# Layer two of a feed-forward block: a sixth Strassen-Winograd product split into seven inner ones, weight differences made together, some sums on GpSimd

## The chip, the cores and the metric

One core of a Trainium2 chip runs the whole program. The metric is device time in microseconds of one launch, the median of several runs. One further execution was taken with the hardware profiler; every duration below is from it.

## The reference

A decoder block on 2048 tokens of width 1024 in float32: an input projection, two token mixers, an output projection, and a feed-forward block. Only the feed-forward block is touched:

```python
hn2 = rmsnorm(h, norm2_g)
up = jnp.einsum('bsd,df->bsf', hn2, w_up)        # 1024 -> 4096
act = jnp.square(jax.nn.relu(up))
h = h + jnp.einsum('bsf,fd->bsd', act, w_down)   # 4096 -> 1024
return rmsnorm(h, final_g)
```

## The kernel before

Precision comes from splitting: `split` writes a high part (ScalarE, a rounding copy) and the remainder (VectorE, a subtraction) of a tile, and each product is three matmuls (high x high, high x low, low x high). One matmul is 128x128 stationary by 128x512 moving.

Both layers use Winograd's form of Strassen's scheme: the matrices are cut in two by two blocks, and seven products P1 to P7 of sums and differences of blocks take the place of eight. The operands on the activations' side are A11, A12, A22, S1, S2, S3, S4; those on the weights' side are b11, b12, b21, b22 and the differences t1, t2, t3 (t1 = b12 - b11, t3 = b22 - b12, t2 = b21 - (b22 - t1), in the kernel's indices).

Layer one (`up`) runs over 32 columns (q, m): q is the half of the tokens, m one of 16 blocks of 128 outputs. A column is seven slots, one product each, of 4 x 3 matmuls into one of the banks X, Y, Z. `make_weights` splits a slot's weights UA = 4 slots ahead, `post` takes the products out of the banks, applies relu and square, and stores the seven operands of layer two, each in `sd[q][i]` (i numbers the operand), by DMAs on SyncE's queue. In the second half of the columns (q = 1), `inner_row` loads the first half's operand again, and `inner_sums` forms inner sums of the operands in INNER and stores them in `sdi[i]`; all of them are made on VectorE. Per pair of columns and operand these are four operations of 128x512: one in the first column (line L886), three in the second (L891, L893, L895).

Layer two (`down`) goes through the products in the order P1, P6, P7, P4, P5, P2, P3. P1, P6 and P3 are plain: 8 blocks of the inner dimension for each half of the tokens, 4 x 6 matmuls each (L1452). P7, P4, P5 and P2 are split again (`SPLIT`): each becomes seven inner products by the same scheme, of 4 steps of 12 matmuls (L1275), so 28 steps and 336 matmuls for 384. A split product needs the inner sums `sdi[i]` of its activation operand (four sums) and the inner differences `wi[i]` of its weight operand (P5, P7, P6, P4), both read back from DRAM. `make` prepares a step ahead: a DMA of the row tile `ar` (128x1024), a split into `ad`, and for each second step a weight tile `wr` or `wq`, split into `wd`; at most six rows and three weight tiles stand ahead of TensorE in the program. The pools hold five `ar` tiles, five `ad` tiles, three `wd` tiles.

Where the weight operands come from: `weights_first` runs in the first half of layer one, a piece at a time at slots chosen by column, and makes first t1 and its inner differences, later t3 and its own, on VectorE (L997, L1003). The rest is made in layer two: the inner differences of b21 (A12) at some steps of P1, P7 and P5, and in P6, where b22 - t1 is P6's own plain weight operand (`minus`, L1166), t2 is made from it, stored, and differenced (L1157). Those run late, through the list `late`.

Instructions of each engine stand in a fixed order that a list scheduler with a time line of its own has set; every engine works through its own order, and so does SyncE's queue, which issues nearly all DMAs. The residual is added by DMAs from GpSimd's queue that accumulate into the result (`add_residual`, L1250).

```python
slots += [c + (s,) for s in ("P2", "P6", "P5", "P7")]
slots += [c2 + ("P1",) for c2 in cols[n + 1:n + 2]]
slots += [c + (s,) for s in ("P4", "P3")]
...
while ahead[0] < limit and (ahead[1] + lefts(ahead[0]) <= 6 and ahead[2] + stationary(ahead[0]) <= 3):
    make(ahead[0])
```

Of the kernel before, what the change touches and what calls it, by code (L numbers as in the profile page):

```python
# [46 lines left out]
def hymba_block(ctx: ExitStack, tc: tile.TileContext, xT, gains, w_in, pool_w, w_out, w_up, w_down, out):  # L47
# [64 lines left out]
    for i in range(PAD):  # L112
# [24 lines left out]
    sdi = {i: [[dram.tile([P, 2, T], F32, name=f"sdi{i}_{n}_{c}") for c in range(4)] for n in range(4)] for i in (1, 2, 3, 5)}  # L137
    wi = {i: {n: [dram.tile([P, 4, 256], F32, name=f"wi{i}_{n}_{c}") for c in range(2)]
              for n in ("P5", "P6", "P7", "P4")} for i in (1, 2, 3, 5)}
    td = [[dram.tile([P, 4, 256], F32, name=f"td{i}_{c}") for c in range(8)] for i in range(3)]  # L140
# [720 lines left out]
    def up(pools, more):  # L861
# [6 lines left out]
        INNER, waiting = (A22, S1, A12, S3), []  # L868

        def inner_row(m, i):  # L870

            if m < NM // 2:
                t = srp.tile([P, 2, T], F32, tag="sr", name="hr") if i != S3 else None
# [4 lines left out]
        def inner_sums(m, i, t, now=False):  # L878
# [12 lines left out]
            nc.vector.tensor_tensor(a, a, t, ALU.add)  # L891
            keep(0, a)
            nc.vector.tensor_tensor(d, t, d, ALU.subtract)  # L893
            keep(1, d)
            nc.vector.tensor_tensor(r, r, d, ALU.subtract)  # L895
# [91 lines left out]
        def weights_first():  # L987

            for i, one, two, keep in ((S1, 1, 0, 0), (S3, 3, 1, 2)):
                for k in range(4):  # L990
                    b = {}
                    for x, y in ((0, 0), (0, 1), (1, 1), (1, 0)):
                        b[x, y], t = (avp.tile([P, 2, 256], F32, tag="av", name=n) for n in ("t1", "b11"))
                        nc.sync.dma_start(t, half(w_down[two, k + 4 * x], y))
                        nc.sync.dma_start(b[x, y], half(w_down[one, k + 4 * x], y))
                        yield
                        nc.vector.tensor_tensor(b[x, y], b[x, y], t, ALU.subtract)  # L997
                        if i == S1 or (x, y) != (0, 1):
                            nc.sync.dma_start(half(td[keep][k + 4 * x], y), b[x, y])
                        for to, u, v, p in {(0, 1): (((0, 0), (0, 1), (0, 0), "P5"),),  # L1000
                                            (1, 1): (((0, 1), (1, 1), (0, 1), "P7"), ((1, 1), (1, 1), (0, 0), "P6")),
                                            (1, 0): (((1, 0), (1, 0), (1, 1), "P4"),)}.get((x, y), ()):
                            nc.vector.tensor_tensor(b[to], b[u], b[v], ALU.subtract)  # L1003
# [114 lines left out]
    def down(pools):  # L1118
# [30 lines left out]
        def inner_weights(i, kk, t):  # L1149

            if kk < 4:
                tops[i] = t
                return
# [490 lines left out]
```

## Time and profile before

| | |
|---|---|
| Median of three runs | 1903.05 us (1901.46 to 1904.54) |
| The profiled execution | 1904.37 us, of which the span from the first to the last instruction is 1902.6 us |
| TensorE busy | 1879.0 us, 99% of the span |
| VectorE busy | 1481.2 us, 78% |
| ScalarE busy | 1025.2 us, 54% |
| GpSimd busy | 179.5 us, 9% |
| DMA | 535.91 MB, mean 282 GB/s |
| Layer one's first matmul, layer two's first | 694.4 and 1309.3 us after the span's start |

Matmuls are pipelined, so 99% busy doesn't mean that no time is lost: the time of a stage against the number of its matmuls tells that. GB/s is what the core's 16 DMA engines moved.

### The profile page before, as it was taken

To read this page: it belongs to the slowest core of one execution; us is meant where nothing else is said; L and a number is where in the kernel's file an instruction comes from. 1 tells how busy PE (TensorE), PEld (TensorE's weight loads), DVE (VectorE), ACT (ScalarE), POOL (GpSimd) and SP (SyncE) were. 2 spreads that over 40 slices of the span, in tenths; PEclk is the share of its full clock that TensorE was granted. 3 is DMA by queue.
4 is the path that set the end of the run, shared out by engine and by line. 5 is a ranking of instruction groups with operands and counts; after the bars stand their busy time and mean duration, and the time that the engine had idled before them with its cause. 6 is when DMAs were issued, how large, how long until landed. Compare 5 with 4: busy or idle time off the path is not lost.

```text
span 1902.6 us, 26763 instructions
## 1 busy us (share of the span) xinstructions
PE 1879.0 (99%) x8947; PEld 1568.1 (82%) x8947; DVE 1481.2 (78%) x2216; ACT 1025.2 (54%) x1616; POOL 179.5 (9%) x399
## 2 busy tenths in 40 slices
PE   9999999999999999999999999999999999999997
PEld 7888888888888888888888888887888888888886
DVE  6887799667966886878799988786666677888774
ACT  5565576555654465454557555554432665656543
POOL 0211123101211030000000000000010010020120
PEclk9999999999999999999999999999999999999998
DMA  6686596788888777787899888889999799999852
GB/s 220 204 273 197 193 297 223 241 311 266 288 314 306 265 266 243 281 313 273 299 359 338 311 293 287 303 282 334 383 314 337 276 317 309 329 300 335 290 209 91
DMA packets 222164, 535.91 MB, mean 282 GB/s; under 512 B 26048, under 2 KB 32192, under 8 KB 218176
## 3 DMA queue, kind: packets, MB, share of 16 engines
q1 hardware_dynamic: 217264, 525.46, 79.3%
q0 software_dynamic: 4608, 8.39, 2.5%
q8 instruction: 72, 1.18, 0.2%
q14 instruction: 76, 0.62, 0.1%
q10 hardware_dynamic: 144, 0.26, 0.0%
HBM read 349.46 MB, written 184.55 MB: 281 GB/s over the span
## 4 chain that ended last, share of the span: by engine, by line
PE 49%; DMA 5%; DVE 3%; ACT 1%; issue 1%; POOL 0%; SPq 0%; DVEq 0%; ACTq 0%
PE pb L1275 13%; PE pY L1102 13%; PE pb L1452 12%; PE pZ L1102 7%; PE pX L1102 3%; DMA ar<-sd 2%; DMA ar<-sdi 1%; PE pb L1392 1%; DMA wr<-in_w_down_dram 0%; DMA b<-in_w_down_dram 0%; DMA t<-in_w_down_dram 0%; DMA td<-t 0%; DMA hn<-hs 0%; DVE hw L147 0%; DMA su<-hs 0%
## 5 line engine op out<-in xcount | busy, mean ns | idle before, releaser
L1102 PE MATMUL pY<-sa,hw 128*128 128x512 f32 x1536 | 366.2, 389 | 1.0 <-ACT u L1025 1.0
L1102 PEld LDWEIGHTS pY<-sa,hw 128*128 128x128 f32 x1536 | 288.0, 188 | 61.8 <-ACT u L1025 2.1
L1275 PE MATMUL pb<-ad,wd 128*128 128x512 f32 x1344 | 305.4, 389 | 0.7 <-DVE ad L147 0.7
L178 PE MATMUL pd<-h,hl 128*128 128x512 f32 x752 | 299.6, 398 | 0.7 <-DVE qkr L424 0.7
L180 PE MATMUL pd<-h,hl 128*128 128x512 f32 x752 | 296.8, 395 | 0.0
L1275 PEld LDWEIGHTS pb<-ad,wd 128*128 128x128 f32 x1344 | 252.1, 188 | 53.9 <-DVE ad L147 1.6
L179 PE MATMUL pd<-h,hl 128*128 128x512 f32 x752 | 296.5, 394 | 0.0
L1452 PE MATMUL pb<-ad,wd 128*128 128x512 f32 x1104 | 253.6, 390 | 1.3 <-ACT ad L146 1.2
L1452 PEld LDWEIGHTS pb<-ad,wd 128*128 128x128 f32 x1104 | 206.6, 188 | 44.7 <-ACT ad L146 1.7
L147 DVE TENSOR_TENSOR ad<-ar,ad 128x1024 fp32r<-128x1024 f32 x160 | 194.2, 1222 | 41.9 <-ACT ad L146 41.3
L146 ACT ACTIVATE ad<-ar 128x1024 fp32r<-128x1024 f32 x160 | 168.3, 1053 | 93.7 <-PE pb L1452 35.4
L1102 PE MATMUL pZ<-sa,hw 128*128 128x512 f32 x768 | 186.5, 389 | 0.8 <-DVE a L1045 0.8
L1102 PEld LDWEIGHTS pZ<-sa,hw 128*128 128x128 f32 x768 | 144.0, 188 | 31.1 <-DVE a L1045 1.2
L178 PEld LDWEIGHTS pd<-h,hl 128*128 128x128 f32 x752 | 142.1, 189 | 28.1 <-DVE qkr L424 1.0
L180 PEld LDWEIGHTS pd<-h,hl 128*128 128x128 f32 x752 | 141.8, 189 | 28.0
L179 PEld LDWEIGHTS pd<-h,hl 128*128 128x128 f32 x752 | 141.8, 189 | 26.9
L146 ACT ACTIVATE hl<-raw 128x512 fp32r<-128x512 f32 x168 | 103.8, 630 | 109.4 <-PE pd L180 70.5
L147 DVE TENSOR_TENSOR hl<-raw,hl 128x512 fp32r<-128x512 f32 x168 | 114.3, 686 | 53.2 <-ACT hl L146 50.1
L1019 ACT ACTIVATE a<-a 128x512 f32<-128x512 f32 x96 | 60.1, 629 | 88.5 <-DVE a L1061 38.1
L147 DVE TENSOR_TENSOR hw<-rt,hw 128x512 fp32r<-128x512 f32 x128 | 86.7, 687 | 24.1 <-ACT hw L146 24.0
L146 ACT ACTIVATE wd<-wq 128x1024 fp32r<-128x1024 f32 x56 | 59.4, 1061 | 79.4 <-PE pb L1275 69.0
L147 DVE TENSOR_TENSOR wd<-wq,wd 128x1024 fp32r<-128x1024 f32 x56 | 68.5, 1224 | 34.3 <-ACT wd L146 34.3
(220 smaller groups left out, 2719.1 us busy)
## 6 DMA issues: line engine op xcount, KB each, us to landing
ar<-sd SPq DMA_DIRECT2D x96, 512.0 KB, 5.9
ar<-sdi SPq DMA_DIRECT2D x64, 512.0 KB, 5.6
rb<-in_w_up_dram SPq DMA_DIRECT2D x30, 1024.0 KB, 6.6
sd<-a SPq DMA_DIRECT2D x104, 256.0 KB, 5.1
raw<-in_w_in_dram SPq DMA_DIRECT2D x50, 512.0 KB, 4.6
sdi<-hr SPq DMA_DIRECT2D x96, 256.0 KB, 5.2
wr<-in_w_down_dram SPq DMA_DIRECT2D x48, 512.0 KB, 5.6
sd<-s SPq DMA_DIRECT2D x88, 256.0 KB, 4.7
```

Of the source, the lines that this page charges most:

```text
L146: nc.scalar.activation(hi, src, AF.Copy)
L147: return nc.vector.tensor_tensor(lo, src, hi.bitcast(F32), ALU.subtract)
L178: nc.tensor.matmul(ps, hl[:, 0, c], hi, start=(k == 0), stop=False)
L179: nc.tensor.matmul(ps, hl[:, 0, c], lo, start=False, stop=False)
L180: mm = nc.tensor.matmul(ps, hl[:, 1, c], hi, start=False, stop=(k == n - 1))
L1019: nc.scalar.activation(t, src, AF.Relu)
L1102: nc.tensor.matmul(t, w[:, wx, c], a[:, ax, c % 2], start=first and c == 0 and x == 0, stop=last and c == G - 1 and x == 2, skip_group_che ...
L1275: nc.tensor.matmul(b, t[:, wx, 2 * (kk % 2) + c, i * P:(i + 1) * P], a[:, ax, c], start=p in ("P1", "P5", "P2") and kk == 0 and c == 0 and ...
L1392: nc.tensor.matmul(b[:, cols], block(t, wx, c, n), a[:, ax, c, cols], start=False, stop=(i == 1 and c == 1 and x == 2), skip_group_check=True)
L1452: nc.tensor.matmul(ps[q, n], block(t, wx, c, n), left_[q][:, ax, c], start=(n_ in ("P1", "P3") and kk == 0 and c == 0 and x == 0), stop=(n ...
```

## The change

P6 is split like the other four. S2 joins INNER, so layer one also makes S2's inner sums; S2's and S3's are made on GpSimd, those of the other three stay on VectorE. `weights_first` now makes t1, t3 and t4 = b22 - t1 from one set of three loads in 16 units (three subtractions on VectorE, then the inner differences of all three on GpSimd). `down` makes t2 = b21 - t4 and the inner differences of b21 and t2 in four units of three parts (load; t2 and b21's; t2's) at the steps of the table TURNS. P1 now leaves both p1 and u2, P6 adds its parts to u2 and copies the sum to u3. The tile pool `avp` has 15 tiles for 13, paid for by one tile less of p1 and of u3; `rtx` is gone.

```diff
-        INNER, waiting = (A22, S1, A12, S3), []
+        INNER, waiting = (A22, S1, A12, S3, S2), []
...
+            engine = nc.gpsimd if i in (S2, S3) else nc.vector
...
-                nc.vector.tensor_tensor(d, d, t, ALU.subtract)
+                engine.tensor_tensor(d, d, t, ALU.subtract)
...
         def weights_first():
+            sub = lambda engine, to, x, y: engine.tensor_tensor(to, x, y, ALU.subtract)
+            KEEP = {S1: 0, S3: 2, S2: 3}
+            for k in range(4):
+                b = {}
+                for x, y in ((0, 0), (0, 1), (1, 1), (1, 0)):
+                    pair = srp.tile([P, 2, 2, 256], F32, tag="sr", name="tw")
+                    t = {S1: pair[:, 0], S3: pair[:, 1], S2: avp.tile([P, 2, 256], F32, tag="av", name="t2")}
+                    for i, at in ((S1, 0), (S3, 1), (S2, 3)):
+                        nc.sync.dma_start(t[i], half(w_down[at, k + 4 * x], y))
+                    yield
+                    sub(nc.vector, t[S1], t[S3], t[S1])
+                    sub(nc.vector, t[S3], t[S2], t[S3])
+                    sub(nc.vector, t[S2], t[S2], t[S1])
+                    for i in (S1, S3, S2):
+                        b[i, x, y] = t[i]
+                        if i == S2 or (x, y) != (0, 1):
+                            nc.sync.dma_start(half(td[KEEP[i]][k + 4 * x], y), t[i])
+                    yield
...
+                            sub(nc.gpsimd, to, u, v)
+                            nc.sync.dma_start(wi[i][p][k // 2][:, 2 * (k % 2):2 * (k % 2) + 2], to)
...
-            if s in (() if n == 0 else SUMS if n < 4 else ("P5", "P4") if n in (5, 7, 9, 11) else
-                     SUMS + ("P6", "P3") if 12 <= n < 16 else ()):
+            if s in (() if n == 0 or n > 13 else ("P2", "P5", "P4", "P3") if n in (3, 11, 12, 13) else ("P5", "P3")):
                 next(first_weights, None)
...
-        SPLIT = {"P7": S3, "P4": A22, "P5": S1, "P2": A12}
+        SPLIT = {"P6": S2, "P7": S3, "P4": A22, "P5": S1, "P2": A12}
...
+        TURNS = {4: (0, 0), 5: (1, 0), 6: (2, 0), 7: (0, 1), 10: (1, 1), 12: (2, 1), 22: (0, 2), 26: (1, 2), 29: (2, 2),
+                 40: (0, 3), 44: (1, 3), 47: (2, 3)}
+        def unit_weights(part, k):
+            sub = lambda to, x, y: nc.vector.tensor_tensor(to, x, y, ALU.subtract)
+            def differences(i, pair):
...
+                    sub(b[to], b[x], b[y])
+                    nc.sync.dma_start(wi[i][p][k // 2][:, 2 * (k % 2):2 * (k % 2) + 2], b[to])
+            if part == 0:
+                for name in ("b21", "t4"):
+                    unit[name] = rlp.tile([P, 2, 4, 256], F32, tag="rl", name=name)
+                    for x in range(2):
+                        nc.sync.dma_start(unit[name][:, x], w_down[2, k + 4 * x] if name == "b21" else td[3][k + 4 * x])
+            elif part == 1:
+                for x in range(2):
+                    sub(unit["t4"][:, x], unit["b21"][:, x], unit["t4"][:, x])
+                    for y in range(2):
+                        if (x, y) != (0, 1):
+                            nc.sync.dma_start(half(td[1][k + 4 * x], y), half(unit["t4"][:, x], y))
+                differences(A12, unit["b21"])
+            else:
+                differences(A22, unit["t4"])
...
-            elif n == "P6":
-                w = minus(blk(b22, kk), blk("t1", kk))
...
-            if n_ in CHAIN:
-                nc.scalar.activation(val(CHAIN[n_], q)[:, n], b, AF.Copy)
-                if n_ == "P6":
-                    nc.scalar.activation(val("u3", q)[:, n], b, AF.Copy)
-                elif n_ == "P1":
-                    add_residual(val("p1", q)[:, n], j0, 0, n)
+            if n_ == "P1":
+                nc.scalar.activation(val("p1", q)[:, n], b, AF.Copy)
+                nc.scalar.activation(val("u2", q)[:, n], b, AF.Copy)
+                add_residual(val("p1", q)[:, n], j0, 0, n)
...
-                    for name in {"P7": ("u3",), "P4": ("c21",), "P5": ("u3", "u2"), "P2": ("p1",)}[n_]:
+                    for name in {"P6": ("u2",), "P7": ("u3",), "P4": ("c21",), "P5": ("u3", "u2"), "P2": ("p1",)}[n_]:
```

Two places in the engines' orders. First VectorE in layer one's second half, before, in the second column of a pair (`hw` are split weights, `rt` weight sums, `hr` loaded rows of the first half, `s1`, `s2`, `a21`, `a12` the operands that `post` makes; numbers tell buffers apart):

```order
L891 TENSOR_TENSOR s1_12212<-s1_12212,s1_12375 128x512
L893 TENSOR_TENSOR hr_12121<-s1_12375,hr_12121 128x512
L1055 TENSOR_TENSOR s2_12384<-s1_12375,a11_12262 128x512
L1057 TENSOR_TENSOR a21_12372<-a11_12262,a21_12372 128x512
L1061 TENSOR_TENSOR a12_12410<-pZ_12291,u2_12286 128x512
L921 TENSOR_TENSOR rt_12512<-rb_12307,rt_12512 128x512
L147 TENSOR_TENSOR hw_12487<-rb_12149,hw_12487 128x512
L147 TENSOR_TENSOR hw_12517<-rb_12307,hw_12517 128x512
L895 TENSOR_TENSOR hr_12121<-hr_12121 128x512
L891 TENSOR_TENSOR a21_12209<-a21_12209,a21_12372 128x512
L893 TENSOR_TENSOR hr_12125<-a21_12372,hr_12125 128x512
```

The same place after, on VectorE:

```order
L892 TENSOR_TENSOR s1_12644<-s1_12644,s1_12809 128x512
L894 TENSOR_TENSOR hr_12550<-s1_12809,hr_12550 128x512
L1065 TENSOR_TENSOR s2_12818<-s1_12809,a11_12695 128x512
L1067 TENSOR_TENSOR a21_12806<-a11_12695,a21_12806 128x512
L1071 TENSOR_TENSOR a12_12850<-pZ_12725,u2_12720 128x512
L922 TENSOR_TENSOR rt_12955<-rb_12741,rt_12955 128x512
L147 TENSOR_TENSOR hw_12930<-rb_12581,hw_12930 128x512
L896 TENSOR_TENSOR hr_12550<-hr_12550 128x512
L147 TENSOR_TENSOR hw_12960<-rb_12741,hw_12960 128x512
```

And what GpSimd's order holds there after, for one pair of columns (GpSimd had nothing in this layer's second half before):

```order
L887 TENSOR_TENSOR hr_12557<-hr_12557,s2_12648 128x512
L887 TENSOR_TENSOR hr_12554<-hr_12554,a21_12641 128x512
L892 TENSOR_TENSOR s2_12648<-s2_12648,s2_12818 128x512
L894 TENSOR_TENSOR hr_12557<-s2_12818,hr_12557 128x512
L892 TENSOR_TENSOR a21_12641<-a21_12641,a21_12806 128x512
L894 TENSOR_TENSOR hr_12554<-a21_12806,hr_12554 128x512
L896 TENSOR_TENSOR hr_12558<-hr_12558,hr_12557 128x512
L896 TENSOR_TENSOR hr_12555<-hr_12555,hr_12554 128x512
```

The operations on `a21` (S3) with the `hr` that go with it have left VectorE's order; they stand on GpSimd's together with as many on `s2` (S2), eight per pair of columns.

Second, VectorE in layer two's P6, before (`ad`, `wd` splits of rows and weights, `wr` plain weight tiles):

```order
L147 TENSOR_TENSOR wd_14573<-wr_14566,wd_14573 128x1024
L147 TENSOR_TENSOR ad_14576<-ar_14569,ad_14576 128x1024
L1157 TENSOR_TENSOR wr_14483<-wr_14483,wr_14404 128x512
L1157 TENSOR_TENSOR wr_14483<-wr_14483 128x512
L147 TENSOR_TENSOR ad_14579<-ar_14570,ad_14579 128x1024
L1166 TENSOR_TENSOR wr_14566<-wr_14582,wr_14566 128x1024
L147 TENSOR_TENSOR wd_14643<-wr_14636,wd_14643 128x1024
L1166 TENSOR_TENSOR wr_14785<-wr_14783,wr_14785 128x1024
L147 TENSOR_TENSOR ad_14646<-ar_14639,ad_14646 128x1024
L147 TENSOR_TENSOR ad_14649<-ar_14640,ad_14649 128x1024
L1166 TENSOR_TENSOR wr_14636<-wr_14652,wr_14636 128x1024
```

And after, in P6, where the third of four units begins:

```order
L147 TENSOR_TENSOR wd_14869<-wq_14867,wd_14869 128x1024
L1169 TENSOR_TENSOR t4_14770<-b21_14767,t4_14770 128x1024 x2
L1169 TENSOR_TENSOR b21_14767<-b21_14767 128x512
L1284 TENSOR_TENSOR u2_14487<-pb_14660,u2_14487 128x512
L1284 TENSOR_TENSOR u2_14487<-pb_14667,u2_14487 128x512
L1169 TENSOR_TENSOR b21_14767<-b21_14767 128x512
L147 TENSOR_TENSOR ad_14822<-ar_14818,ad_14822 128x1024
L147 TENSOR_TENSOR wd_14914<-wq_14911,wd_14914 128x1024
L1169 TENSOR_TENSOR b21_14767<-b21_14767 128x512
L147 TENSOR_TENSOR ad_14827<-ar_14825,ad_14827 128x1024
L147 TENSOR_TENSOR ad_14874<-ar_14870,ad_14874 128x1024
L1169 TENSOR_TENSOR b21_14767<-b21_14767 128x512
```

Before, VectorE's order in P6 holds one weight split for two row splits, with the weights' work among them. After, there are additions of banks to `u2` and a unit's work on `b21` and `t4`, between splits of which there are 42 in the product for 24.

More of the change, by code (lines that the diff above doesn't have):

```diff
@@ L1228, in make @@
                 left_[q] = row([P, 2, 2, T], F32R, "ad", align_bytes=256)
-                last[1] = split((left_[q][:, 0], left_[q][:, 1]), rows[q])
-            while late and n != "P1":
-                late.pop(0)()
-            late.append(lambda: more_weights(n, kk, w))
+                split((left_[q][:, 0], left_[q][:, 1]), rows[q])
             made[g] = t, left_
@@ L1411, in last_steps @@
                 behind.pop(0)()
-        free, held, ahead, late, last = 4, [], [0, 0, 0], [], [None, None]
+        free, held, ahead, last = 4, [], [0, 0, 0], [None]
         def block(t, x, c, n):
@@ L1461, in down @@
             make_ahead()
-            while len(late) > (3 if n_ == "P1" else 0):
-                with tc.issue_after(last[0].ins), tc.issue_after(last[1].ins):
-                    late.pop(0)()
             if n_ == "P3":
```

87 lines of the change are left out of this document (28 added, 59 removed).

## The prediction

> **What bounds the kernel now.** I read the page's first part, then where TensorE's products of the feed-forward block begin and end, then busy time by stage, then the groups and the DMA.
>
> ```profile
> PE 1879.0 (99%) x8947; PEld 1568.1 (82%) x8947; DVE 1481.2 (78%) x2216; ACT 1025.2 (54%) x1616; POOL 179.5 (9%) x399
> 887.11 2.72 PE pX L1102 x12
> 906.15 2.72 PE pX L1102 x12
> L1452 PE MATMUL pb<-ad,wd x1104: 387/389/504, 1309.5 to 1875.9; 128*128 128x512 f32 x184
> L1275 PE MATMUL pb<-ad,wd x1344: 388/389/499, 1485.5 to 1791.3; 128*128 128x512 f32 x192
> ```
>
> A column of the first layer is 7 products of 12 matmuls; two columns begin 906.15 - 887.11 = 19.04 us apart, 0.2267 us a matmul (2.72 us for 12). In layer two, P1 and P6 (8 x 2 x 24 = 384 matmuls each) run from 1309.5 to 1485.5: 176.0 us where 768 x 0.2267 = 174.1 us would do. The four products split in seven (336 each) run to 1791.3: 305.8 us where 304.7 would do. So TensorE bounds the kernel with about 3 us of gaps in layer two, and the rest of this text asks who could open new ones. Stages, with PE, PEld, DVE, ACT, POOL busy us (instructions), clock, DMA share and GB/s:
>
> ```profile
> 887.11:963.27 76.16, 76.16 (x337) 63.06 (x337) 59.17 (x97) 40.39 (x72) 0.00 (x0) 1.00 0.87 307
> 992.50:1020.00 27.50, 27.50 (x124) 22.75 (x122) 27.50 (x41) 19.41 (x31) 0.00 (x0) 1.00 1.01 364
> 1077.51:1267.91 190.40, 190.40 (x841) 157.66 (x841) 158.97 (x259) 101.73 (x180) 0.00 (x0) 1.00 0.85 292
> 1309.50:1396.60 87.10, 85.80 (x377) 70.39 (x376) 54.96 (x58) 32.51 (x35) 4.28 (x5) 1.00 0.98 357
> 1396.60:1485.50 88.90, 88.90 (x393) 73.60 (x393) 50.30 (x51) 32.70 (x40) 2.88 (x4) 1.00 0.97 334
> 1561.90:1638.40 76.50, 76.50 (x339) 63.36 (x338) 62.76 (x65) 46.33 (x49) 1.76 (x2) 1.00 0.93 323
> 1735.00:1762.50 27.50, 27.04 (x119) 22.07 (x118) 27.50 (x30) 20.49 (x23) 0.00 (x0) 1.00 0.96 342
> ```
>
> The rows are four columns of layer one's first half, a stretch at its middle, ten columns of its second half, P1, P6, P4 and a stretch of P2. VectorE is the next limit: it was busy all 27.5 us from 992.5 with no matmul lost (124 records), and all 27.5 us from 1735 with about four lost (119), 0.9 us. DMA is third.
>
> **TensorE's part of the change.** P6 becomes seven inner products: 28 steps x 12 = 336 matmuls for 384. 48 x 0.2267 = 10.9 us go. Nothing else on TensorE changes, so this is the whole of what can be won, save the few us of old gaps.
>
> **Layer one: weights and sums.** Groups, with count, busy us, mean ns:
>
> ```profile
> L997 DVE TENSOR_TENSOR t<-t,b 128x512 f32<-128x512 f32 x32 | 22.0, 692 | 34.7 <-DMA t<-in_w_down_dram 31.6 <-issue 2.5 <-DMA hn<-hs 0.3
> L1003 DVE TENSOR_TENSOR t<-t,t 128x512 f32<-128x512 f32 x32 | 22.1, 689 | 3.3 <-DMA td<-t 3.0
> L895 DVE TENSOR_TENSOR hr<-hr 128x512 f32<-128x512 f32 x32 | 21.5, 686 | 0.0
> masks.py:199 POOL TENSOR_SCALAR_AFFINE_SELECT ident<-ident 128x128 f32<-128x128 f32 x1 | 0.3, 284 | 0.0
> L660 POOL COPY left<-pc x56: 182/534/2977, 95.7 to 519.1; 128x2 f32<-128x2 f32 x56
> L214 POOL TENSOR_SCALAR v<-v x18: 192/193/6377, 62.4 to 1851.4; 128x4 int32<-128x4 int32 x18
> ```
>
> VectorE: 32 differences (L997) become 48; the 32 inner ones (L1003) and the 32 inner sums of S3 go to GpSimd, which gets 48 inner differences and 64 inner sums, 112 operations of 128x512. No row shows such an operation there. The nearest give bounds: 128x128 with one input took 284 ns, two elements 182 at least, so 0.81 ns an element: 0.6 us for 512 with one input, 1.0 us if two inputs are read in turn. I take 1.0. That GpSimd has time is plain (112 us of 32 columns, 609 us). What matters is whether it takes VectorE's: L660 shows 182 ns of work in a median of 534 and up to 2977 while VectorE is busy, L214 up to 6377, so the two do get in each other's way, at least one way round.
>
> If every GpSimd operation stopped VectorE for its whole length: the ten columns have 158.97 us for 259 operations, 0.614 each. S3's sums take away 4 per pair of columns, 20: 146.7 us remain. 40 GpSimd operations add 40.0: 186.7 of 190.4, it fits, up to 1.09 us an operation. In the four columns from 887.11, 24 operations of the old schedule become 21 on VectorE (seven units of three) and 21 on GpSimd: 59.17 - 1.8 + 21.0 = 78.4 us for 76.16, and the 2.2 us over are covered: weights are split four slots ahead, 4 x 2.72 = 10.9 us. So GpSimd's load costs nothing by this sum. What is left is the queues: SyncE now waits for GpSimd's results before it stores them, and loads stand behind (the next column's weights, asked for two columns, 38 us, ahead; the rows hn, which VectorE consumes soon). Bounds 0 to 3 us for that, since L997 above shows VectorE already waiting 31.6 us for loads in this stage with almost nothing lost; I take 1.5.
>
> The Trainium skill, GPSIMD Engine Reference, section 3.1, has a two-input add of 2048 elements at 4497 ns; an estimate from it is 1.12 us for 512. By it the ten columns would need 191.5 us instead of 186.7, and the second half of the layer would fall some 2 us behind, inside the same cover. No run here shows such an operation yet.
>
> **Layer two: VectorE and DMA while P6 and P7 run.**
>
> ```profile
> L147 DVE TENSOR_TENSOR ad<-ar,ad 128x1024 fp32r<-128x1024 f32 x160 | 194.2, 1222 | 41.9 <-ACT ad L146 41.3
> L1283 DVE TENSOR_TENSOR u<-pb,u 128x512 f32<-128x512 f32 x42 | 26.4, 683 | 0.0
> L1157 DVE TENSOR_TENSOR wr<-wr 128x512 f32<-128x512 f32 x32 | 22.1, 690 | 21.3 <-DMA td<-wr 11.6 <-DMA wr<-in_w_down_dram 9.3
> L1166 DVE TENSOR_TENSOR wr<-wr 128x1024 f32<-128x1024 f32 x16 | 19.5, 1221 | 11.4 <-DMA wr<-td 6.0 <-DMA ar<-sd 3.0 <-DMA wr<-in_w_down_dram 1.6
> L146 ACT ACTIVATE ad<-ar 128x1024 fp32r<-128x1024 f32 x160 | 168.3, 1053 | 93.7 <-PE pb L1452 35.4 <-PE pb L1275 22.8 <-DMA ar<-sd 18.4
> L1256 ACT ACTIVATE u<-pb x8: 578/598/617, 1476.8 to 1485.7; 128x512 f32<-128x512 f32 x8
> ```
>
> An inner product has 28 row splits and 14 weight splits of 1.22 us and 14 additions of 0.683: 60.8 us (P4's row shows 62.76 with leftovers). To P6 come the units k = 1 and 2 by the new table: 4 differences of 1.22 and 16 of 0.69, 15.9 us. Together 76.7 us of durations in 336 x 0.2267 = 76.2 us: VectorE is full in P6. P7 has one unit, 68.8 us. P1 is light (24 splits and one unit, 37 of 87 us), so VectorE enters P6 a full lead ahead, the five split tiles: 5 x 2.72 = 13.6 us. But it must not wait: the rows L1157 and L1166 waited 32.7 us in 48 operations; the same share for the 20 in P6 is 13.6 us, just the lead. ScalarE has 42 x 1.05 + 8 x 0.6 = 49 us there, no limit; the copies of P6's end (u2 and u3, 16) become 8 at P1's end and 8 in P6, at no cost, since P6's first two banks are done with by TensorE 36 matmuls, 8.2 us, before P6 starts, and four copies take 2.4.
>
> DMA in P6: 28 rows and 14 weight tiles of 524 KB, 22.0 MB; the stores of unit 1 (11 x 262 KB, 2.9), loads and stores of unit 2 (2.1 + 2.9), the eight additions of the residual to P1's result (2.1): 32.0 MB in 76.2 us is 420 GB/s. P7: 22.0 + 5.0 + 2.1 = 29.1 MB. What was held for a whole product is 357 GB/s (P1) and 334 (P6). At 357, P6 needs 89.6 us and P7 81.5: 13.4 + 5.3 = 18.7 us late at the end. The lead is ten row tiles, five raw and five split, 27.2 us, less landing and splits:
>
> ```profile
> ar<-sd SPq DMA_DIRECT2D x96, 512.0 KB, 5.9
> ```
>
> 27.2 - 5.9 - 1.05 - 1.22 = 19.0 us. So at 357 nothing is lost, at 334 (19.6 + 10.9 = 30.5 us late) 11.5 us. Both limits meet in the same 76 us; I take 4 of the 0 to 11.5.
>
> Freed: eight operations L1166 and the second load of each b21 block. They lay in P1 and P6, where VectorE had 32 us and more spare in a product: nothing. The 4 KB of tiles moved about in layer one (p1 and u3 kept once) cost nothing while VectorE adds them to a bank within a slot.
>
> **Sum.** -10.9 + 1.5 + 4 = -5.4 us. The profiled execution took 1904.4 us, the median of the runs is 1903.05; taken from the median, 1897.6 us. From no change one can tell about 0.2%, 3.8 us.
>
> **Rivals.** (a) *Slower: GpSimd holds VectorE.* If an operation stops VectorE for t > 1.09 us, the second half of layer one (64 operations) loses 64 x (t - 1.09) less the 10.9 us cover. All that is won is gone from t = 1.37 on (17.8 / 64 above 1.09); at 1.5 it is 26.2 - 10.9 = 15.3 us there and 57.4 + 31.5 - 76.2 - 10.9 = 1.8 in the four columns: -10.9 + 17.1 + 4 = +10, 1913 us. For it: L660 and L214, stretched many times over. Against: those rows show GpSimd waiting, and none of the 128x512 groups quoted shows VectorE above 0.692 us. The Trainium skill, SBUF — State Buffer, section "Who interferes with whom", makes this a rule: an exclusive lock on a shared port, between GpSimd reading SBUF and a VectorE operation with two SBUF inputs. The stretched rows agree that someone waits; that VectorE does, no run here shows.
> (b) *P6 and P7 saturate.* DMA at 334 GB/s: -10.9 + 11.5 + 1.5 = +2, 1905 us. For it: a DMA share of 0.97 in P6 already. Against: no matmul lost there.
> (c) *All is won.* Neither stage falls behind: 1903.05 - 10.9 = 1892.2. For it: 992.5, VectorE full and nothing lost.
>
> **Chances.** Forecast (1893.5 to 1899.2) 0.42; all won 0.16; (b) and what lies between, 1899.2 to 1906.9, 0.20; (a) 0.17; other ways to more than that 0.05. Faster 0.58, same 0.20, slower 0.22. The range goes from 1891.5 (all won and a few tenths of old gaps) to 1908, which leaves out most of (a).
>
> **What would show it.** In the profile after: 336 matmuls of the seven inner products for P6, 76 to 80 us from P6's start to P7's; layer one still 19.04 us a column; GpSimd's 128x512 operations near 1 us; VectorE's 128x512 groups at 0.69. Columns longer than 19.3 us with VectorE groups above 0.8 would be (a); TensorE waiting for ad tiles in P6 or P7, landing times of 10 us and more, (b). I am wrong if the gaps lie elsewhere: at the change from layer one to two, where P1's rows stand behind GpSimd's last sums on SyncE.

## The result, and the profile after

The changed kernel takes 1933.65 us (1932.17 to 1934.56) where 1897.6 was forecast; against the kernel before the ratio is 1.0158 (95% interval 1.0143 to 1.0173). It is 1.6% slower, clear of the noise, and outside the range given.

The profiled execution took 1932.3 us, its span 1930.5. From the page's first part, and from the answers for the three lines of matmuls (count, ns, first and last start):

```profile
PE 1877.8 (97%) x8899; PEld 1556.4 (81%) x8899; DVE 1565.6 (81%) x2192; ACT 1040.2 (54%) x1634; POOL 376.6 (20%) x511
L1111 PE MATMUL pY<-sa,hw x1536: 387/389/499, 692.8 to 1331.9; 128*128 128x512 f32 x192
L1455 PE MATMUL pb<-ad,wd x720: 387/389/692, 1335.4 to 1903.7; 128*128 128x512 f32 x180
L1276 PE MATMUL pb<-ad,wd x1680: 387/389/504, 1428.5 to 1819.5; 128*128 128x512 f32 x187
```

The 48 matmuls are gone (1104 + 1344 = 2448 before, 720 + 1680 = 2400 now). Three stretches follow from these rows, the first two from a first start to the next, the third from its own first start to its last: layer one 692.8 to 1335.4 = 642.6 us (614.9 before, worked out in the same way), P1 93.1, the 1680 inner matmuls (the split products) 391.0 where 1680 x 0.2267 = 380.9 would do. P1 and the split products together took 484.1 us, 2.3 more than the 176.0 + 305.8 of before, although 10.9 were saved: 13.2 us were lost there. With 27.7 us in layer one that is 30.0; layer one started 1.8 us earlier and the end was 0.3 shorter, which leaves 27.9, the difference of the spans.

Who made TensorE wait (the waits of PE, each line in us, times, longest):

```profile
PE pX L1111 <- DVE hw L147: 9.9, 8, 1.8
PE pZ L1111 <- DVE hw L147: 7.5, 8, 1.1
PE pb L1276 <- DVE ad L147: 6.9, 8, 2.3
PE pb L1455 <- DVE ad L147: 4.2, 1, 4.2
PE pY L1111 <- ACT u L1035: 4.1, 5, 1.1
```

In layer one it waits for split weights `hw`, eight times in each of two banks: once or so per pair of columns. In layer two it waits for rows `ad`. The stages side by side, six pairs of columns of the second half, after and then before (columns as in the prediction):

```profile
1064.07:1310.36 246.29, 233.47 (x1009) 189.48 (x1009) 221.49 (x289) 121.82 (x216) 87.08 (x49) 0.99 0.87 302
```
```profile
1058.31:1286.78 228.47, 228.47 (x1009) 189.19 (x1008) 194.16 (x317) 121.92 (x217) 0.00 (x0) 1.00 0.86 297
```

For the same 1009 matmuls 246.3 us instead of 228.5: a pair of columns takes 41.0 us for 38.1. VectorE has 28 operations fewer and is busy 27 us longer. Its groups in about that stretch, and its and GpSimd's timeline through one burst of GpSimd's operations (start, duration):

```profile
L147 DVE TENSOR_TENSOR hw<-rb,hw 128x512 fp32r<-128x512 f32 x36 | 41.2, 1146 | 0.7 <-ACT hw L146 0.7
L147 DVE TENSOR_TENSOR hw<-rt,hw 128x512 fp32r<-128x512 f32 x48 | 38.8, 818 | 10.3 <-ACT hw L146 10.3
L924 DVE TENSOR_TENSOR rt<-rb,rt 128x512 f32<-128x512 f32 x12 | 20.2, 1684 | 0.0
L1055 DVE TENSOR_TENSOR a<-pZ,u 128x512 f32<-128x512 f32 x12 | 8.2, 685 | 5.9 <-ACT u L1035 5.9
```
```profile
1098.32 0.68 DVE L1071 TENSOR_TENSOR a<-pZ,u 128x512 f32<-128x512 f32 x1
1098.92 1.18 DVE L922 TENSOR_TENSOR rt<-rb,rt 128x512 f32<-128x512 f32 x1
1100.03 1.78 DVE L147 TENSOR_TENSOR hw<-rb,hw 128x512 fp32r<-128x512 f32 x1
1101.73 1.78 DVE L896 TENSOR_TENSOR hr<-hr 128x512 f32<-128x512 f32 x1
1103.43 1.77 DVE L147 TENSOR_TENSOR hw<-rb,hw 128x512 fp32r<-128x512 f32 x1
...
1108.51 0.68 DVE L892 TENSOR_TENSOR a<-a,a 128x512 f32<-128x512 f32 x1
```
```profile
1097.93 1.62 POOL L892 TENSOR_TENSOR s<-s,s 128x512 f32<-128x512 f32 x1 [15.34 <-issue]
1099.51 1.75 POOL L894 TENSOR_TENSOR hr<-s,hr 128x512 f32<-128x512 f32 x1
1101.22 1.73 POOL L892 TENSOR_TENSOR a<-a,a 128x512 f32<-128x512 f32 x1
1102.92 1.73 POOL L894 TENSOR_TENSOR hr<-a,hr 128x512 f32<-128x512 f32 x1
1104.60 3.44 POOL L896 TENSOR_TENSOR hr<-hr 128x512 f32<-128x512 f32 x2
```

The two engines take turns: while GpSimd works through six operations, VectorE ends one every 1.70 us, 1.78 long instead of 0.68, and GpSimd ends one every 1.7 as well. Of each turn 0.6 us are VectorE's (its pace alone, from 1108.51 on) and 1.1 GpSimd's. The addition L1055, one of whose inputs is a PSUM bank, keeps its 0.685.

### The profile page after: what moved, and what is told of

Same layout as the page of the kernel before. It is cut to its first block, busy times and chain, and to the rows that moved or that the text cites. A ratio compares the mean times of both kernels' runs of the same rounds, so it can differ in the third digit from the quotient of the medians.

```text
span 1930.5 us, 27002 instructions
## 1 busy us (share of the span) xinstructions
PE 1877.8 (97%) x8899; PEld 1556.4 (81%) x8899; DVE 1565.6 (81%) x2192; ACT 1040.2 (54%) x1634; POOL 376.6 (20%) x511
## 5 line engine op out<-in xcount | busy, mean ns | idle before, releaser
L1276 PE MATMUL pb<-ad,wd 128*128 128x512 f32 x1680 | 384.3, 390 | 7.0 <-DVE ad L147 6.9
L1276 PEld LDWEIGHTS pb<-ad,wd 128*128 128x128 f32 x1680 | 314.4, 188 | 76.8 <-DVE ad L147 11.7
L147 DVE TENSOR_TENSOR ad<-ar,ad 128x1024 fp32r<-128x1024 f32 x172 | 208.5, 1225 | 37.0 <-ACT ad L146 36.7
L146 ACT ACTIVATE ad<-ar 128x1024 fp32r<-128x1024 f32 x172 | 178.8, 1051 | 73.1 <-PE pb L1276 18.3
L1455 PE MATMUL pb<-ad,wd 128*128 128x512 f32 x720 | 167.7, 393 | 4.2 <-DVE ad L147 4.2
L180 PEld LDWEIGHTS pd<-h,hl 128*128 128x128 f32 x752 | 141.4, 188 | 27.9
L1455 PEld LDWEIGHTS pb<-ad,wd 128*128 128x128 f32 x720 | 135.7, 189 | 32.7 <-DVE ad L147 4.6
L146 ACT ACTIVATE wd<-wq 128x1024 fp32r<-128x1024 f32 x70 | 74.2, 1060 | 103.8 <-PE pb L1276 87.4
L147 DVE TENSOR_TENSOR hw<-rt,hw 128x512 fp32r<-128x512 f32 x128 | 106.2, 836 | 20.2 <-ACT hw L146 20.2
L147 DVE TENSOR_TENSOR wd<-wq,wd 128x1024 fp32r<-128x1024 f32 x70 | 85.6, 1222 | 45.2 <-ACT wd L146 44.9
```

The source lines that it names most:

```text
L146: nc.scalar.activation(hi, src, AF.Copy)
L147: return nc.vector.tensor_tensor(lo, src, hi.bitcast(F32), ALU.subtract)
L180: mm = nc.tensor.matmul(ps, hl[:, 1, c], hi, start=False, stop=(k == n - 1))
L1276: nc.tensor.matmul(b, t[:, wx, 2 * (kk % 2) + c, i * P:(i + 1) * P], a[:, ax, c], start=p in ("P1", "P5", "P2") and kk == 0 and c == 0 and ...
L1455: nc.tensor.matmul(ps[q, n], block(t, wx, c, n), left_[q][:, ax, c], start=(n_ in ("P1", "P3") and kk == 0 and c == 0 and x == 0), stop=(n ...
```

## The experiments

All are short edits of the changed kernel or of the one before. The ratio is to the kernel before on the same chip. Stretches in us, one profiled execution each: layer one, P1 (first plain to first inner matmul), the inner products.

| kernel | median (runs) | ratio, interval | layer one | P1 | inner |
|---|---|---|---|---|---|
| after | 1933.65 (5) | 1.0158 (1.0143 to 1.0173) | 642.6 | 93.1 | 391.0 |
| sums_vector | 1916.98 (2) | 1.0064 (1.0042 to 1.0086) | 627.5 | 93.6 | 390.8 |
| all_vector | 1913.23 (6) | 1.0043 (1.0018 to 1.0069) | 627.2 | 94.0 | 390.4 |
| s2_pool | 1916.75 (7) | 1.0056 (1.0037 to 1.0075) | 628.9 | 89.3 | 391.8 |
| no_unit_subs | 1914.8 (1) | | 624.9 | 95.3 | 388.4 |
| no_s2_sums | 1912.59 (1) | | 624.1 | 91.1 | 390.5 |
| no_units | 1896.4 (1) | | 620.9 | 88.3 | 381.5 |
| no_s2_no_units | 1899.05 (1) | | 624.3 | 87.1 | 381.4 |
| later_units | 1916.12 (3) | 1.0074 (1.0051 to 1.0097) | 622.9 | 95.7 | 393.9 |
| a12_later | 1918.3 (3) | 1.0073 (1.005 to 1.0096) | 624.9 | 93.6 | 394.3 |
| all_vector_rows | 1926.08 (4) | 1.011 (1.0093 to 1.0127) | 648.8 | 89.8 | 381.9 |
| p5_first_late | 1917.84 (4) | 1.0066 (1.0044 to 1.0089) | 624.9 | 93.8 | 392.8 |
| p5_spread | 1906.42 (10) | 1.0006 (0.9995 to 1.0016) | 624.3 | 87.8 | 388.8 |
| p5_spread2 | 1912.85 (6) | 1.0051 (1.0036 to 1.0066) | 619.3 | 88.4 | 395.2 |
| p5_spread3 | 1907.11 (12) | 1.0019 (1.0007 to 1.0031) | 622.7 | 87.0 | 390.9 |

A single kernel's runs lie up to 15 us apart (all_vector 1907.4 to 1922.1), so differences of a few us between single stretches say little.

### What GpSimd costs

**all_vector** puts all of the change's GpSimd operations back on VectorE, **sums_vector** the 64 inner sums alone.

```diff
-            engine = nc.gpsimd if i in (S2, S3) else nc.vector
+            engine = nc.vector
...
-                            sub(nc.gpsimd, to, u, v)
+                            sub(nc.vector, to, u, v)   # all_vector only
```

> The changed kernel with every operation it gave to GpSimd (48 inner weight differences, 64 inner sums) done on VectorE. Theory H (a GpSimd operation stops VectorE's operations with two inputs in SBUF for about 1.1 us each): VectorE's stretched groups go back to 0.69 us, the second half of layer one goes back from 40.97 to about 38.1 us per pair of columns, layer one from 642.6 to about 616 us, and the time falls by 25 to 30 us to 1903 to 1909. Rival W (the work itself is too much, whoever does it: 56 operations of 0.61 us a pair): the pairs stay above 40 us, the time above 1925. Rival L (the loss is in layer two): layer one stays about as it is and the time above 1925.

> The changed kernel with only the 64 inner sums of S2 and S3 back on VectorE; the 48 inner weight differences stay on GpSimd in layer one's first half. Theory H with the first half as measured (its sixteen columns lost only some 2.6 us): nearly as good as with everything on VectorE, 1905 to 1911. Rival: if SyncE's queue waiting behind GpSimd's results does the harm, the first half, where it waits for 48 of them, keeps several us: above 1913.

Both take some 15 us off layer one (642.6 to 627.2 and 627.5), and nothing off layer two. The 64 sums of the second half are the whole of it; the 48 differences of the first half, spread over 16 columns, cost nothing in the end. But all_vector, with no GpSimd operation in this layer, still takes 12 us more than before: the expectation, 616 us for the layer and 1903 to 1909 in all, had put the whole loss on GpSimd.

**before_pool_reads** and **before_pool_writes** add 64 pieces of GpSimd work to the kernel before, in the second half, on a scratch tile that nobody reads.

```diff
                 marks["S3"] = put(S3, t)
+                if q:
+                    for _ in range(2 if m < NM // 2 else 6):
+                        nc.gpsimd.tensor_tensor(sslast, k[S2], rlast[:, 0], ALU.subtract)   # reads
+                        # writes: tensor_copy of one element of k[S2], then two memsets of sslast
```

> The kernel before with 64 GpSimd subtractions added in layer one's second half, two behind P4 of the first column of a pair and six behind P4 of the second, each reading S2's tile and a constant tile and writing a scratch tile that nobody reads. Nothing is taken from VectorE, and no transfer waits for them. Theory H: VectorE has 31.8 us of work a pair and gets 8 x 1.1 = 8.8 of stops, 40.6 us: pairs of 40.6 to 43 us, 20 to 40 us slower than before. Rival Q (SyncE's queue behind GpSimd does the harm): no more than 2 us slower, pairs at 38.1.

> As the one that reads, but in place of each of the 64 subtractions GpSimd copies one element a partition from S2's tile and then fills a scratch tile of 128x512 with zeros twice, so it is as busy but reads next to nothing. If the stop comes through reading SBUF (what the stretched groups say, which all read two tiles): pairs at 38.1 to 38.6 us and less than 4 us slower than before. If any GpSimd access to SBUF stops VectorE: 15 us slower or more.

The first took 1942.6 us, layer one 648.8 (+33.9), 42.2 us a pair of columns; the second 1900.0, layer one 615.1, 38.1 a pair. Groups of the first, then of the second (second half, count | busy, mean ns):

```profile
L1061 POOL TENSOR_TENSOR sslast<-s,rlast 128x512 f32<-128x512 f32 x64 | 108.7, 1699 | 532.7 <-DVE s L1055 529.0
L147 DVE TENSOR_TENSOR hw<-rb,hw 128x512 fp32r<-128x512 f32 x33 | 35.8, 1087 | 0.0
```
```profile
L1063 POOL MEMSET sslast<- 128x512 f32 x128 | 67.5, 527 | 7.5
L147 DVE TENSOR_TENSOR hw<-rb,hw 128x512 fp32r<-128x512 f32 x37 | 25.3, 686 | 4.8 <-ACT hw L146 3.3 <-DMA sdi<-hr 1.4
```

No DMA waits for either kind, so stores that stand behind GpSimd on SyncE's queue are not what costs. Reading two inputs stops VectorE, 128 writes of whole tiles don't. This is the rule that the prediction gave from the Trainium skill, SBUF — State Buffer, section "Who interferes with whom": a VectorE operation with two SBUF inputs is blocked by a GpSimd instruction that reads SBUF, and by none that only writes. The traces agree: a mean of 1.087 us for `hw` beside the reads, up to 1.78 for 0.68 in the changed kernel, 0.686 beside the writes.

**s2_pool** leaves S2's 32 sums alone on GpSimd, four a pair of columns for eight.

> The changed kernel with everything on VectorE but the 32 inner sums of S2, which stay on GpSimd: four GpSimd operations a pair of columns for eight. Theory A (the sum decides: 31.9 us of VectorE's own work and 4 x 1.1 of stops, 36.3 us a pair, fits into 38.1): pairs at 38.1 us. Theory F (VectorE cannot use the some 4 us a pair in which it waits for ScalarE; with eight stops it was busy 36.9 us of 41.0): 36.3 + 4 = 40 us a pair and 10 to 16 us slower than with everything on VectorE, about 1923 to 1929.

1916.75 us, level with all_vector's 1913 within what its runs allow; columns of the last six pairs are irregular, 39.7 us a pair in the mean (38.5 in all_vector), though its layer one is only 1.7 us longer. By the busy times four operations should have fitted; it isn't plain that all of it does.

### Layer two and the end of layer one

**no_unit_subs** makes no subtractions in the units (their transfers stay), **no_s2_sums** no inner sums of S2, **no_units** no units at all, **no_s2_no_units** neither; all from all_vector.

```diff
-                    sub(b[to], b[x], b[y])                                  # no_unit_subs, with t4's
-        INNER, waiting = (A22, S1, A12, S3, S2), []                         # no_s2_sums
+        INNER, waiting = (A22, S1, A12, S3), []
-            if g in TURNS:                                                  # no_units
-                unit_weights(*TURNS[g])
```

> Everything on VectorE, and layer two's weight units (b21, t2) without their subtractions: all their loads and stores remain, VectorE has 15.9 us less to do in P6 and 8 us less in P7. Leaves out the subtractions, so stores hold undiffered weights. Theory V (VectorE, full in P6, opens the gaps of P6 and P7): the 336 x 2 matmuls of P6 and P7 lose under 2 us instead of some 7. Theory D (DMA at 380 to 411 GB/s does): they still lose 4 us or more.

> Everything on VectorE, and S2's inner sums left out in layer one (neither loaded, made nor stored); P6's inner products read S3's sums in their place. Leaves out S2's sums, so P6 multiplies other rows; the bytes that P6 reads are the same. Theory B (S2's extra loads and stores crowd the DMA at the end of layer one and the start of P1): layer one goes from 627.2 to 615 to 619 us and P1, first plain to first inner matmul, from 94.0 to 87 to 90; P6 and P7 lose what they lost. Rival: the losses there come from the new order or from the weight units in P1: layer one 623 and more, P1 92 and more.

> Everything on VectorE, and layer two's weight units left out altogether (no loads, subtractions or stores, 20 MB); P4 and P2 read S3's and S1's weights in their place. Leaves out t2 and the inner differences of b21 and t2. Theory D (the bytes crowd P6 and P7): the 1680 inner matmuls take 381 to 384 us instead of 390.4; P1 falls too, to 87 to 91, for as much as the first unit is in its way. If theory B is the whole of P1's loss, P1 stays at 93 to 95. Rival: P6 and P7 lose their time to the rows and splits of an inner product as such, 389 and more.

> Both left out. If bytes are all that stands against the 48 matmuls saved, the whole gain appears: layer one 615 to 618, P1 87 to 88, inner products 381 to 383, the time 10 us below the kernel before, some 1892 to 1896. If it stays above 1900, something else in the change costs time.

The units as a whole are worth 5.7 us in P1 and 8.9 in the inner products: without them these lose next to nothing (88.3 for 87.1, 381.5 for 380.9). Most of it is their 20 MB of transfers. With these and without the subtractions P1 takes 95.3 us, and P6, counted off by its 336 matmuls, 82.8 us for all_vector's 82.7, where 76.2 would do. Only P7 gains, 76.2 for 79.3, and there the units' last loads had also come earlier, behind 29 row loads for 39. The 6.3 us by which layer one differs can't be put down to the units' transfers: all_vector issues their first load at 1324.3, when layer one is over (1319.6), and between no_s2_sums and no_s2_no_units they make no difference (624.1, 624.3). Nor is a price of S2's sums shown: without them layer one is 3 us shorter beside the units and 3 us longer without the units. P1 and the second and third of the pieces of 40 us behind it, of no_units and of all_vector (columns as in the prediction):

```profile
1313.00:1401.30 88.30, 87.89 (x385) 71.84 (x385) 42.68 (x45) 36.23 (x43) 5.64 (x7) 1.00 0.81 287
1441.30:1481.30 40.00, 40.00 (x178) 33.12 (x177) 31.64 (x31) 26.24 (x31) 0.00 (x0) 1.00 0.88 289
1481.30:1521.30 40.00, 40.00 (x178) 33.12 (x177) 30.45 (x29) 22.05 (x23) 0.00 (x0) 1.00 0.85 290
```
```profile
1319.60:1413.60 94.00, 90.00 (x385) 73.99 (x384) 56.88 (x63) 36.35 (x43) 5.62 (x7) 0.96 0.97 360
1453.60:1493.60 40.00, 35.85 (x150) 27.25 (x149) 30.64 (x32) 22.41 (x27) 0.00 (x0) 1.00 0.97 369
1493.60:1533.60 40.00, 37.51 (x164) 30.20 (x163) 32.51 (x36) 20.06 (x22) 0.00 (x0) 1.00 0.93 343
```

In the piece from 1453.6 all_vector loses 28 of 178 matmuls, at 369 GB/s for 289, with 30.6 us of VectorE, fewer than no_units has in its own. These shares don't say what is late. TensorE waits there for splits `ad` of VectorE; ScalarE waits for rows only 5.8 us in P6 and P7 together, and from 1482 to 1500 VectorE goes through splits and the last unit's subtractions without a pause. So that the units' transfers cost P6 its time is shown by leaving out the rest; by what way they make a split late is not.

**later_units** sets the units to later steps (5 to 52 for 4 to 47). **a12_later** moves b21's differences to P4 and P5 besides and loads b21 again. **p5_first_late** runs P5 ahead of P4, so that t2 is due a product later, and spreads the units over steps 8 to 80.

```diff
-        TURNS = {4: (0, 0), 5: (1, 0), 6: (2, 0), 7: (0, 1), ...
+        TURNS = {8: (0, 0), 10: (1, 0), 12: (2, 0), 16: (0, 1), ...      # p5_first_late
-        order = (("P1", A11), ("P6", S2), ("P7", S3), ("P4", A22), ("P5", S1), ("P2", A12))
+        order = (("P1", A11), ("P6", S2), ("P7", S3), ("P5", S1), ("P4", A22), ("P2", A12))
```

> Everything on VectorE, and the table of the weight units spread evenly: steps 5, 7, 8; 12, 17, 20; 28, 33, 36; 44, 49, 52, with three to five steps between a load and its use. Theory: the 4 to 6 us lost at P1's start come from a unit's subtractions that stand in VectorE's order before their load has landed, so they go down by 3 us or more; P6 and P7 keep losing some 5 us, since the bytes are the same. Time 1903 to 1910.

> As the evenly spread table, and the inner differences of b21 (A12) taken out of the units and made in P4 and P5 (loads at steps 64, 75, 86, 97), where the DMA moved 285 to 300 GB/s and no matmul was lost. P6 and P7 have 1.05 MB and 2.8 us of VectorE less per unit, at the price of loading b21 twice. Both V and D: P6 and P7 lose under 3 us; 1899 to 1906. If P4 and P5 then lose matmuls, DMA is full there too.

> all_vector with layer two's products in the order P1, P6, P7, P5, P4, P2, P3, so that t2 and its inner differences are due 76 us later, and the parts of the four units spread over P1 to P5 (steps 8 to 80 for 4 to 47). Nothing is left out. From layer one's first matmul to the last inner one all_vector took 627.2 + 94.0 + 390.4 = 1111.6 us, without the units 1090.7. Theory D (the units' 20 MB are too much for the stretch from layer one's end to P7 at what a core moves there): spread over one more product most of the 21 us come back, 1092 to 1099 us from first to last, a median of 1894 to 1901, faster than the kernel before. Rival T (the bytes cost their time wherever they stand, as later_units and a12_later suggest): 1108 to 1114 us, 1910 to 1916.

None gained anything, and for a reason that the table does not show. The loads of a unit's b21 in all_vector, later_units and p5_first_late (ns, first and last issue):

```profile
L1182 SPq DMA_DIRECT2D b<-in_w_down_dram x8: 332/333/1470, 1324.3 to 1463.0; - x8
```
```profile
L1182 SPq DMA_DIRECT2D b<-in_w_down_dram x8: 332/520/1308, 1323.3 to 1461.3; - x8
```
```profile
L1181 SPq DMA_DIRECT2D b<-in_w_down_dram x8: 333/333/1289, 1325.3 to 1461.8; - x8
```

They had not moved: the scheduler, it seems, puts a load on SyncE's queue when its tile is free, wherever the program has it. In all three kernels the loads stand behind 4, 11, 25 and 38 or 39 row loads `ar`; those of a12_later came earlier, behind 4, 6, 21 and 29, and b21's second loads behind 44 to 64, still ahead of P7's end. These runs say nothing about a later place. (p5_first, with only the last two units set later, kept its places too: 1915.95 us.)

**all_vector_rows** gives layer one's rows `hr` one buffer more for two tiles less of `avp`, against the waits of their loads at its end; **no_s2_no_units_rows** does the same in no_s2_no_units.

```diff
-        rba, srp = spool("rba", 1), spool("srp", SR)
+        rba, srp = spool("rba", 1), spool("srp", SR + 1)
-... spool("rbb", 1), spool("avp", 15)
+... spool("rbb", 1), spool("avp", 13)
```

> all_vector with the pool srp one tile larger (SR + 1, 4 KB) and avp two tiles smaller (13 for 15): the rows hr of A22, S1 and A12 have one more buffer, so their loads need not wait on SyncE for the last stores of the old hr; nothing is left out. Theory R (layer one's end is late because hr loads wait for stores out of the same tile, SPq L876 <- DMA sdi<-hr): layer one takes 617 to 621 us for all_vector's 627.2, the median is 1904 to 1907. Rival O (the end is late because VectorE has S2's 32 sums more and its order there is full): 625 to 629 us, 1911 to 1916. Rival V (two tiles of avp less stop the operands and S2's rows instead): over 630 us, above 1917.

> The same two pool sizes in no_s2_no_units, which leaves out S2's inner sums (P6 reads S3's) and the weight units (P4 and P2 read other differences). VectorE's work in layer one's second half is then that of the kernel before. Theory R: layer one 615 to 618 us for 624.3, the time 1889 to 1893. Rival O gives nothing here, since S2's sums are not made: 624 us, 1899. If layer one stays at 624 with the extra rows, what makes the end late is neither VectorE's work nor these buffers.

As a test of the buffers this failed: the pools' places in SBUF moved too, and layer two's first tiles now came free late (the first row is PE's longest wait in all_vector_rows). It showed something else. The second row is a piece of P6 that is to be set beside all_vector's from 1453.6:

```profile
PE pb L1455 <- ACT wd L146: 35.5, 1, 35.5
```
```profile
1473.40:1513.40 40.00, 40.00 (x179) 33.10 (x178) 32.23 (x32) 26.23 (x31) 0.00 (x0) 1.00 0.91 313
```

After a pause of 35.5 us, in which transfers went on, the same units cost 2.7 us in P1 and 1.0 in the inner products. When P1 began, ten row loads had been issued, in all_vector three. And the units had gone by: here their loads stand behind 4, 10, 15 and 21 row loads, the last at 1410.3, 23 us ahead of P6; in all_vector the last is issued 49 us into P6. This agrees with time for the units' bytes being what is short; no run gave it without a pause. Rows are not short when P6 begins: in both kernels nine row loads had then been issued, counting the row in use, and four rows were split. no_s2_no_units_rows took 1913.3 us with layer one at 635.7, for the same reason; the buffers' own part stays open.

**p5_spread** binds the queue itself: each part of a unit stands on SyncE behind the row load of the step before it, with P5 ahead of P4. **p5_spread2** and **p5_spread3** are other tables for the same code.

```diff
-                unit_weights(*TURNS[g])
+                with tc.issue_after(last_row[0].ins):
+                    unit_weights(*TURNS[g])
...
-            nc.sync.dma_start(r, {"P1": sd[0][i][kk], ...
+            last_row[0] = nc.sync.dma_start(r, {"P1": sd[0][i][kk], ...
```

> The order P1, P6, P7, P5, P4, P2, P3 again, and now each part of a unit stands on SyncE's queue behind the row load ar of the step before it (in later_units, a12_later, p5_first and p5_first_late the queue's order had kept the units at the same 52 row loads as in all_vector, whatever the table said). By the queue's order the loads of the four units now come after 12, 20, 40 and 68 row loads, for 4, 11, 25 and 39 in all_vector. Nothing is left out. Theory D (the 20 MB in the stretch from layer one's end to P7 cost 21 us): layer one 620 to 623 us, P1 88 to 91, the inner products 382 to 386, the median 1894 to 1901. Rival T (the bytes cost their time wherever they stand): the sum of the three stays at 1108 to 1114 us, 1910 to 1916.

> As p5_spread, the units later and evenly apart: their loads after 14, 26, 48 and 70 row loads, each unit's parts spread over 14 steps and more. Theory D: as p5_spread or 1 to 3 us better, since no two units meet; 1892 to 1900. Rival T: 1910 to 1916. If p5_spread is at 1896 and this one above 1903, the b21 and t4 tiles held longer, or the last unit before P4, have a price of their own.

> As p5_spread with the units' loads after 14, 22, 36 and 54 row loads for 12, 20, 40 and 68: the first as late as in p5_spread2 (whose layer one took 619.3 us for 624.3), the last before the residual is added to P7's result (where p5_spread lost 5 us, at 1560 to 1600). Nothing is left out. Theory D: layer one 619 to 622, P1 88, the inner products 382 to 387, together 1089 to 1097 for p5_spread's 1100.9; the median 1894 to 1902, faster than the kernel before. Rival: the stretch that is full is only moved to P6, the inner products take 390 or more, 1905 to 1910.

In p5_spread, P1, a piece of P6, the piece from P7's end into P5 (which begins at 1557.8), and the loads of b21:

```profile
1317.00:1404.80 87.80, 87.61 (x385) 71.91 (x384) 54.39 (x60) 36.36 (x43) 5.60 (x7) 1.00 0.98 367
1444.80:1484.80 40.00, 40.00 (x178) 33.14 (x177) 35.07 (x39) 24.12 (x29) 0.00 (x0) 1.00 1.03 405
1524.80:1564.80 40.00, 37.93 (x164) 30.81 (x163) 34.55 (x37) 22.48 (x26) 7.00 (x8) 0.98 1.05 366
L1181 SPq DMA_DIRECT2D b<-in_w_down_dram x8: 333/422/426, 1345.8 to 1525.4; - x8
```

Now the units moved, their last loads by 62 us, and P1's loss of 6 to 7 us is gone in all three kernels, although p5_spread's DMA moved 367 GB/s in P1 and all_vector's 360. So it matters where they stand. A piece of P6 ran at 405 GB/s without losing a matmul; the loss came behind P7, in P5 (83.7 us for 76.2), where the last unit meets the additions of the residual. p5_spread3 has its last unit ahead of those and lost in P7 instead (84.4, and 78.2 in P6). The inner products lose 8 to 14 us in all three: theory D holds for P1, the rival for the products behind it. p5_spread is level with the kernel before, 7 us below all_vector; p5_spread3 is 0.2% above. No complete version is faster than before.

## Why the prediction was wrong

- **TensorE, -10.9:** right. P6 has 336 matmuls, and 48 x 0.2267 came off.
- **A GpSimd operation, taken at 1.0 us between 0.6 and 1.0:** the least in the trace is 1.29 us, about 1.7 while VectorE works:

```profile
L990 POOL TENSOR_TENSOR tw<-tw x32: 1290/1645/5292, 735.1 to 987.8; 128x512 f32<-128x512 f32 x32
L896 POOL TENSOR_TENSOR hr<-hr x16: 1708/1732/1739, 1063.4 to 1347.4; 128x512 f32<-128x512 f32 x16
```

  The estimate from the Trainium skill, GPSIMD Engine Reference, section 3.1 (1.12 us) was nearer, and still 13% under the least.
- **"It fits, up to 1.09 us an operation":** this is the step that failed. VectorE is stopped 1.78 - 0.68 = 1.1 us by an operation, right at that bound, and yet the sums cost 15 us. The step added busy times over ten columns and took every idle microsecond of VectorE as usable. In the six pairs it was busy 221.5 us, less than the 228.5 they had taken before, and idle for the other 24.8: about 4 us a pair in which it waited for ScalarE (`hw`, `u`, `a`), which GpSimd's turns don't fill. And six operations in a row take 10 us, during which VectorE does six operations for some sixteen; the "four slots ahead", 10.9 us, were not there in this burst. That shape is read from the timeline; s2_pool, with half the operations, supports it but doesn't settle it.
- **Rival (a):** its mechanism was the right one, its place too. Its price, 64 x (t - 1.09) - 10.9, gives nothing at the measured 1.1 and 28 us at the whole 1.7; 15 were measured. That the traces of before showed no VectorE group above 0.692 was no evidence against it, as GpSimd had nothing to read there.
- **The four columns of the first half, "covered":** right in sum (627.5 with, 627.2 without GpSimd's 48 differences).
- **Queues in layer one, 1.5 (0 to 3):** mis-sized. With no GpSimd operation layer one is still 12.3 us longer than before. GpSimd's sums on SyncE are not the cause, and the units' transfers start only behind the layer (in all_vector at 1324.3, 4.7 us after its end). By the first matmuls of the columns, all_vector takes 4.0 us less than before over the first sixteen columns, 6.3 more over the next four and 10.0 more over the last two (51.8 for 41.8). The last two vary most, down to 42.7 in p5_spread2, and are at 49.5 with S2's sums and the units both left out. What makes these columns long stays open.
- **P1:** the prediction gave it no loss: "P1 is light (24 splits and one unit, 37 of 87 us)". For VectorE it was (56.5 of 93.1 us, with two units); the queue's order put two units behind 4 and 5 of P1's rows, and 6 us went. Leaving out the subtractions gains nothing there (95.3); with the first unit behind 12 or 14 rows the loss is gone (87.0 to 88.4).
- **P6 and P7, 4 (0 to 11.5):** 8.9 measured (79.7 and 81.6 us for 76.2 each), near the upper end. The rate was not overrated: P6 moved 381 GB/s, P7 343, pieces of 15 us up to 411. The lead was there too, nine row loads issued and four rows split when P6 began, counting the row in use. By the sum that had to be enough at 357 GB/s. It wasn't: 44 us later five were issued and none was split through, and near the waits in P7 (at 1508.2, 1521.5 and 1532.9) three or four rows had landed and again none was split through. So a lead of row tiles does not pay for lateness as the sum had it. Near those waits VectorE works without a pause from 1507 to 1520, yet P6 loses as much without the units' subtractions (no_unit_subs); which of the two limits takes how much in the complete kernels stays open.
- **The sum:** -10.9 + 1.5 + 4 was forecast. Measured: -10.9, 15.4 by GpSimd, 12.3 in layer one without it, 13.2 in P1, P6 and P7; 30.0 in all.

The places named under what would show it were the right ones, columns above 19.3 us with VectorE above 0.8, waits for `ad` in P6 and P7, gaps at the change of layers. All three came at once, where the chances had treated them as alternatives.

## What to carry to other kernels

Busy times that add up to less than the stage's length don't show that it fits: take off the idle time that is waiting, and set the longest burst against the lead that is there. Where a stage begins with only a few tiles loaded, further transfers cost time in its first microseconds that they don't cost a few loads later (P1: 94.0 us in all_vector, which issues its first unit's loads 5 us after P1's start, 89.3 in s2_pool, 13 us after, 87.0 to 88.4 with 29 to 33 us). And before reading an experiment that moves work, look at the times in its trace: a scheduler that works by its own time line may have kept everything in place.

## What was not expected of the hardware

- VectorE's operations with two inputs in SBUF and GpSimd's alternate one by one, neither gets ahead: 1.70 us for one of each, 0.6 and 1.1.
- 128 whole-tile memsets on GpSimd at 0.527 us each left VectorE's groups at 0.686.
- The core's DMA held 405 GB/s for 40 us with TensorE losing nothing, and a stage's mean rate says little about whether a row is late: 360 GB/s in P1 went with 6 us lost in all_vector, 367 with none in p5_spread.
